# The lower part of streamed weights: a negative rounded copy by ScalarE and an adding transfer, in place of a subtraction by GpSimd

## The chip, the cores and the metric

The kernel runs on one core of one Trainium2 chip. The metric is the device time of one execution in microseconds (us). Three executions of the kernel before took 3351.83, 3354.24 and 3357.93 us; the median is 3354.24 us. Differences of about 0.2% (6.7 us) can be told apart.

## The reference

The kernel computes a small hybrid network for one sequence of 512 tokens of width 1024, in float32. It has two blocks of two layers each. Cut to what matters here:

```python
# block 1, two layers: two attentions side by side, then a gated feed forward with a convolution
h = rms_norm(x, attn_pre_gain);  u = h @ w_in                  # queries, keys, values, gates
o_a = swa_sink_attention(...)                                  # sliding window
o_b = nsa_attention(...)                                       # compressed, selected and window keys
mixed = sigmoid(g_a) * (o_a @ w_branch_a) + sigmoid(g_b) * (o_b @ w_branch_b)
x = x + rms_norm(mixed @ w_out, attn_post_gain)
h = rms_norm(x, ffn_pre_gain)
x = x + rms_norm(conv_ffn(h, w_up, conv_w, conv_b, w_down), ffn_post_gain)

def conv_ffn(h, w_up, conv_w, conv_b, w_down):                 # w_up: 1024 x 5632, w_down: 2816 x 1024
    u = h @ w_up
    c = conv_b + sum(conv_w[k] * shift(u, 2 - k) for k in range(3))
    a, val = split(c, 2);  return (gelu(a) * val) @ w_down

# block 2, two layers: a projection w_in_2, a convolution of width 7 over tokens and silu, a scan over the
# sequence in both directions in chunks of 128 tokens (ssd_chunked), a windowed attention, w_out_2, and the
# same kind of feed forward
```

Nearly all of the arithmetic is products of activations (512 tokens) with weight matrices. The weights are read once each.

## The kernel before

**Two parts of every number.** TensorE multiplies in a format that holds about half of a float32's significant bits (float32r in the program). So each weight is split into an upper part `wh`, the weight rounded to that format, and a lower part `wl = w - wh`; activations are split into `h` and `hl` (`ah` and `al` in the feed forward's second product) in the same way. A product of a 128x128 tile of weights with a 128x512 tile of activations is three matmuls into one PSUM bank, in `mm3`: L488 (`wh` by `h`), L489 (`wl` by `h`) and L490 (`wh` by `hl`).

**The stream of weights.** All weights lie in HBM in the order in which the kernel uses them (a table, PLAN), in 460 chunks of eight tiles: 128 partitions by 1024 float32, 512 KB. A class Stream takes them one after another. When the first tile of chunk c is asked for (`next`, L337), it first issues loads of raw chunks up to number c + 6 on SyncE's DMA queue (`load`, L301; four buffers `raw`), and then the conversions up to chunk c + 3 (`conv`; four buffers each of `wh` and `wl`). A conversion writes `wh` by a ScalarE copy that rounds (L314), or in the attention stages, 60 chunks of the 460, by a GpSimd cast (L312), since ScalarE is busy with exponentials there; then GpSimd subtracts: L315, `wl = raw - wh`. A chunk is 24 matmuls.

**The order.** Every engine works through its own list in the order in which the program's text issues the work, and waits where an operand isn't there. Other work is put between the matmuls by hand: `W.defer(n, f)` runs f after n more tiles of weights. So the place of the conversions in ScalarE's and GpSimd's lists is set by the calls of `next`.

**What the other engines do beside it.**
- Norms: ScalarE squares each of eight tiles (L416), VectorE adds them in turn (L421, the last one L424), TensorE sums over features with a column of ones (L433, `stat`). `dense_group` computes four output tiles of the next product meanwhile. L402 (ScalarE) and L403 (VectorE) make the two parts of the activations. After a post norm L1341 adds to x, on VectorE and GpSimd in turn.
- Feed forward: 22 pairs of output tiles of `w_up` in each of the four layers; 66 chunks of weights a layer, those of `w_down` among them. Each tile is evacuated by VectorE (L1224, `u`), convolved by ScalarE (L1228) and twice by VectorE (L1229, L1231); each pair then takes a gelu (L1250, ScalarE), a product (L1293, VectorE) and the split into `ah` (L1296, ScalarE) and `al` (L1298, VectorE). After thirteen pairs comes the first half of `w_down`.
- Block 2's convolution: GpSimd adds one tap (L1410), VectorE five (L1416), ScalarE applies silu (L1421), and TensorE transposes the result (L1520, `xtp`).
- The scan: GpSimd builds masked decays (L1628, `adm`) and weighted tiles (L1544, L1643, L1684), TensorE multiplies them (L1658, `gp`), VectorE forms the mixing tiles (L1662 to L1671), adds to the result (L1695, `xd`) and applies the gate z (L1704).
- Attention: scores on TensorE, exponentials on ScalarE (`p`, L1084 in block 1, L1938 in block 2), transposes of them on TensorE (L673, `pt`). In block 1 the gates of the branches are transposed once a layer (L1024, `gnt`, from `gn`, evacuated by VectorE at L811).

Of the kernel before, what the change touches and what calls it, by code (L numbers as in the profile page):

```python
# [23 lines left out]
NSLOT = 66              # working tiles of 128 x T  # L24
NB, NO = 2, 2           # output tiles taken together where the last factor comes late
XD = 30                 # tiles of weights before the first heads' queries are split
GA, GB, GC = 1, 4, 1    # tiles of weights before, between and within the gated products
NWU, NKW = 13, 6        # products that keep the clock up: at the start, at a norm
# [6 lines left out]
# ------------------------------------------------------------------ weight stream  # L35
# [8 lines left out]
def _plan():  # L44
    """128x128 weight tiles in the order in which the tensor engine takes them."""
# [103 lines left out]
# ------------------------------------------------------------------ constants of the shapes  # L149
# [37 lines left out]
def _onehot():  # L187
    """Bucket of each relative position -255..255 (t5, bidirectional); row 32 marks the outside."""
    oh = np.zeros((33, 512), np.float32)
    for i in range(512):  # L190
        rel = i - 255
        if i == 511 or abs(rel) > 128:
            oh[32, i] = 1
            continue
        n = abs(rel)
        b = n if n < 8 else 8 + sum(n * n >= 64 * 2 ** k for k in range(1, 8))
        oh[(16 if rel > 0 else 0) + min(b, 15), i] = 1
    return oh
# [48 lines left out]
def trunk_kernel(ctx: ExitStack, tc: tile.TileContext, xT, positions, wts, cst_d, oh_d, rb_d, cw1_d,  # L247
# [20 lines left out]
    # the eight banks of PSUM in turn; a bank that is held stays out until it is free again  # L268
# [16 lines left out]
    # ---------------------------------------------------------------- weights  # L285
    class Stream:
# [18 lines left out]
        def conv(self, upto):  # L305
            while self.conved < min(upto, NCHUNK):
# [3 lines left out]
                lo = wpool.tile([128, CH * 128], F32R, tag="wl", name="wl", bufs=4)  # L310
                if busy["act"]:
                    G.tensor_copy(h, r)  # L312
                else:
                    A.activation(h, r, AF.Copy)  # L314
                G.tensor_sub(lo, r, h.bitcast(F32))  # L315
# [3 lines left out]
        def defer(self, n, fn):  # L319
            """fn after n more tiles of weights."""  # L320
            self.later.append((self.t + n, fn))
# [26 lines left out]
        def drip(self, gen):  # L348
            """One step of gen for each tile of weights from now on."""
# [7 lines left out]
    # ---------------------------------------------------------------- constants  # L357
# [38 lines left out]
    def split(h, lo, src, eng_l=None, scale=None):  # L396
        """h + lo == src (times the column scale), each in 12 significant bits."""
# [7 lines left out]
    class Squares:  # L405
        """Squares summed over the feature tiles; the last tile stays one of its own where it comes late."""
# [19 lines left out]
        def sums(self, upto):  # L426
            """The sums over the features of a tile, [token of a block, block], for the tiles that are there."""
# [9 lines left out]
    def rstd_a(sq, n, act=False):  # L437
        """1/sqrt(mean + eps) of each token, [token of a block, block]."""
# [19 lines left out]
    def warm_sqrt():  # L458
        """Brings the table of the square root in ahead of its use."""
        A.activation(small(1, "warm"), epst, AF.Sqrt)  # L460

    def keep_warm(n):
        """Products that keep the tensor engine's clock up while it waits."""
# [4 lines left out]
    def spread(r4):  # L468
        """[token of a block, block] to [any partition, token], in PSUM."""
# [22 lines left out]
    def dense(keys, hs, evac):  # L492
        """One output tile; yields after each tile of the contraction."""
# [12 lines left out]
    def dense_parts(keys, hs, cut, evacs):  # L506
        """Some output tiles: the first part of the contraction for each of them, then the rest."""
# [11 lines left out]
    def dense_group(keys, hs, evacs, sq, store, x=None, after=None):  # L519
        """Four output tiles, the contraction outermost: it starts with the first tile of hs.  The factor of the  # L520
        norm (of the squares sq, of x where they are still to come) and what follows from it come a little into
        the next product."""
# [30 lines left out]
    def prep(x, gcol, late=False):  # L553
        """Gain and split of a tile, and its square for the norm; as a function of the tile's number."""
# [32 lines left out]
    def run_units(units, lags, fill, per, tail=0, prep=()):  # L587
        """Stage k of unit u comes at step u + lags[k]; the filler goes in between (per: steps per unit, tail:
        steps of the filler for each step after the last unit; prep: pieces of work, each with its first step)."""
# [25 lines left out]
    def pieces_of(gen, n):  # L615
        """A generator's n pieces as functions."""
        return [lambda: next(gen, None)] * n

    def stack_q(X, h, get):
        """One of a pair of heads as a tile of its two parts: products over all 128 rows; in two pieces."""  # L620
# [7 lines left out]
    def stack_k(K, g, get):  # L628
        """Keys of one of a pair of groups: their upper part and their lower part, each twice; in four pieces."""
# [19 lines left out]
    def head_units(h, score, ranges, order, vt, o, final):  # L649
        """The four units of a head: the scores of each block of queries; then for each block of keys (ranges: the  # L650
        queries that see it) the probabilities transposed, in two parts, and their product with the two parts of
        the values, side by side, over all those queries at once.  order: the keys, such that each of these
        products either adds to sums of all its queries or, the bank's marks cleared by the first one, starts them
        all.  o["t"][its half] becomes the
        product, [features, tokens]."""
# [57 lines left out]
    def widen(o, den):  # L713
        """A factor of each token, [token of a block, block and head], for each feature."""
# [3 lines left out]
    def spread_pair(o):  # L718
        """A pair of heads, [features, tokens], times their factors."""
# [11 lines left out]
    def value_parts(pt, s, name):  # L731
        """Values of one of a pair of groups, [tokens of a block, block, upper and lower part]."""
# [10 lines left out]
    # ================================================================ block 1  # L743
# [39 lines left out]
    def layer1(l, x, hs, sq, gnext, side):  # L783
# [48 lines left out]
        def tokens(src, name):  # L832
            """[features, tokens] to [tokens of a block, block, features]."""
# [5 lines left out]
        # ---- compressed keys and values  # L839
        cmp = {}  # L840

        def windows(src):
            """The tokens 16 n + 2 i + (0 or 1) of each group of heads, with the position added."""
# [70 lines left out]
        def cmp_scores(i):  # L914
            """Softmax over the compressed blocks, times the gate, transposed; all heads of a block."""
# [42 lines left out]
        def head(src, h):  # L958
            """The two pieces that make head h's tile; the source goes after the second head of the pair."""
# [7 lines left out]
        # ---- projections  # L967
# [63 lines left out]
        # ---- fillers  # L1031
# [20 lines left out]
        # ---- attention units  # L1052
# [10 lines left out]
        def halves(name):  # L1063
            """Half a tile; the other half goes to the next call."""
# [6 lines left out]
        def score_of(h, X, K, mask, k0, init, nm, den, last):  # L1071
            """Exponentials of the scores of a block of queries, not yet normed, and their first block of keys."""
# [16 lines left out]
        # sliding window with sinks  # L1089
# [42 lines left out]
        # selected blocks (all of them are selected) and window, both causal  # L1132
# [41 lines left out]
        # ---- branches, output, post norm  # L1174
# [40 lines left out]
        # ---- feed forward  # L1215
# [85 lines left out]
    def later(i, gated):  # L1301
        """The gated products of the pairs that are there, in steps a little into the products that follow."""
# [4 lines left out]
    class Acts:  # L1307
        """Eleven of the gated products, each taken when it is there."""
# [702 lines left out]
```

## Time and profile before

| | |
|---|---|
| median of three executions | 3354.24 us |
| span of the profiled execution | 3354.5 us |
| TensorE matmul (PE) busy | 3132.5 us, 93% |
| VectorE (DVE) busy | 2145.5 us, 64% |
| ScalarE (ACT) busy | 1465.3 us, 44% |
| GpSimd (POOL) busy | 1539.9 us, 46% |
| the 16 DMA engines, SyncE's queue | 303.50 MB, 28.7% of their time |
| read from HBM | 275.64 MB |

The span of the profiled execution is the time from its first to its last instruction and stands for the whole of it; it lies 0.3 us above the median. PE is TensorE's matmuls, PEld its loading of weights, SP is SyncE, which issues the loads of weights. Busy time is the time during which an engine executed something; time in which an instruction is held up after it has begun counts as busy. In rows "L315 POOL TENSOR_TENSOR wl<-wraw,wh" means: the instruction of line 315, on GpSimd, that writes `wl` from `wraw` and `wh`. A tile name of one letter, as `c`, `x` or `u`, is the working tile that the program calls so.

### The profile page before, as it was taken

The numbers are of one execution on the slowest core, as the hardware profiler recorded it, in microseconds if no ns is written. First come the engines' busy times: TensorE is split into PE (matmuls) and PEld (weight loads), VectorE is DVE, ScalarE is ACT, GpSimd is POOL, SyncE is SP. The second block draws the span as 40 slices with busy tenths as digits, with TensorE's granted clock in tenths as the row PEclk, the third lists the DMA queues.
The fourth block names the chain that finished last, engine by engine and source line by source line (L and its number), as shares of the span: only waits on it lengthen the run. The fifth ranks groups of instructions, "written<-read, shape, count | busy, mean of one in ns | idle before, by whom it ended". The sixth has DMA issues, their size and how long they took to land. (4 is left out here: it accounts for less than half of the span.)

```text
span 3354.5 us, 39917 instructions
## 1 busy us (share of the span) xinstructions
PE 3132.5 (93%) x14604; PEld 2567.9 (77%) x14604; DVE 2145.5 (64%) x3431; ACT 1465.3 (44%) x2828; POOL 1539.9 (46%) x770
## 2 busy tenths in 40 slices
PE   9989989999989999999888889999998888999998
PEld 7778778887778877888766667888887666788887
DVE  7787467263887747635578987462528898836253
ACT  3357344343246634433345466342333545734232
POOL 4533434554534334544447543354444664335443
PEclk8999999999999999999898899999999989999999
DMA  5311333333521133333321121333332102133332
GB/s 191 101 45 45 101 106 95 107 114 113 164 67 48 48 129 91 102 100 126 104 71 55 46 72 57 109 105 124 93 128 67 57 32 82 57 107 101 126 94 69
DMA packets 104031, 306.05 MB, mean 91 GB/s; under 512 B 12651, under 2 KB 21867, under 8 KB 103836
## 3 DMA queue, kind: packets, MB, share of 16 engines
q1 hardware_dynamic: 103836, 303.50, 28.7%
q8 instruction: 116, 1.90, 0.2%
q14 instruction: 79, 0.65, 0.1%
HBM read 275.64 MB, written 19.96 MB: 88 GB/s over the span
## 5 line engine op out<-in xcount | busy, mean ns | idle before, releaser
L315 POOL TENSOR_TENSOR wl<-wraw,wh 128x1024 fp32r<-128x1024 f32 x460 | 1165.2, 2538 | 1075.6 <-ACT wh L314 1006.4
L488 PE MATMUL acc<-h,wh 128*128 128x512 f32 x2464 | 1005.2, 408 | 0.7 <-ACT h L402 0.7
L489 PE MATMUL acc<-h,wl 128*128 128x512 f32 x2464 | 978.2, 397 | 2.5 <-POOL wl L315 2.5
L490 PE MATMUL acc<-hl,wh 128*128 128x512 f32 x2464 | 976.5, 396 | 0.2
L314 ACT ACTIVATE wh<-wraw 128x1024 fp32r<-128x1024 f32 x400 | 418.9, 1051 | 357.3 <-PE acc L490 257.9
L490 PEld LDWEIGHTS acc<-hl,wh 128*128 128x128 f32 x2464 | 473.1, 192 | 104.7 <-DVE hl L403 1.8
L489 PEld LDWEIGHTS acc<-h,wl 128*128 128x128 f32 x2464 | 474.6, 193 | 98.4 <-POOL wl L315 5.3
L488 PEld LDWEIGHTS acc<-h,wh 128*128 128x128 f32 x2464 | 475.0, 193 | 96.1 <-issue 5.0
L488 PE MATMUL acc<-ah,wh 128*128 128x512 f32 x704 | 274.4, 390 | 0.0
L490 PE MATMUL acc<-al,wh 128*128 128x512 f32 x704 | 274.1, 389 | 0.0
L489 PE MATMUL acc<-ah,wl 128*128 128x512 f32 x704 | 273.9, 389 | 0.0
L673 PE MATMUL pt<-cst,p 128*128 128x128 f32 x752 | 143.1, 279 | 34.1 <-DVE nm L1936 13.4
L1416 DVE SCALAR_TENSOR_TENSOR c<-u,prm,c 128x510 f32<-128x510 f32 (+2 forms) x120 | 147.9, 1233 | 40.8 <-POOL c L1410 37.4
L312 POOL CAST wh<-wraw 128x1024 fp32r<-128x1024 f32 x60 | 70.4, 1173 | 207.7 <-PE acc L490 207.5
L1298 DVE TENSOR_TENSOR al<-c,ah 128x512 fp32r<-128x512 f32 x88 | 118.0, 1341 | 70.8 <-ACT ah L1296 70.8
L490 PEld LDWEIGHTS acc<-al,wh 128*128 128x128 f32 x704 | 132.2, 188 | 28.5 <-DVE al L1298 0.9
L488 PEld LDWEIGHTS acc<-ah,wh 128*128 128x128 f32 x704 | 132.2, 188 | 27.8 <-ACT ah L1296 0.6
L489 PEld LDWEIGHTS acc<-ah,wl 128*128 128x128 f32 x704 | 132.2, 188 | 27.1
L421 DVE TENSOR_TENSOR sq<-sq 128x512 f32<-128x512 f32 x81 | 94.5, 1193 | 89.9 <-ACT sq L416 89.9
L1228 ACT ACTIVATE c<-u,prm 128x512 f32<-128x512 f32 x88 | 71.2, 815 | 163.8 <-DVE u L1224 163.8
L1084 ACT ACTIVATE p<-p,nm 128x128 f32<-128x128 f32 x192 | 102.5, 534 | 90.1 <-DVE nm L1082 88.2
L1296 ACT ACTIVATE ah<-c 128x512 fp32r<-128x512 f32 x88 | 55.5, 630 | 195.3 <-DVE c L1293 195.3
(333 smaller groups left out, 5313.7 us busy)
## 6 DMA issues: line engine op xcount, KB each, us to landing
wraw<-in_wts SPq DMA_DIRECT2D x460, 512.0 KB, 3.6
bias<-bias_d SPq DMA_DIRECT2D x32, 192.0 KB, 2.4
x<-in_xT SPq DMA_DIRECT2D x16, 256.0 KB, 6.1
cw<-in_cw SPq DMA_DIRECT2D x16, 256.0 KB, 4.4
xf<-x SPq DMA_DIRECT2D x16, 256.0 KB, 2.2
x<-xf SPq DMA_DIRECT2D x16, 256.0 KB, 5.6
xs<-x SPq DMA_DIRECT2D x16, 256.0 KB, 3.5
x<-xs SPq DMA_DIRECT2D x16, 256.0 KB, 6.0
```

Source lines behind the costliest of these rows:

```text
L312: G.tensor_copy(h, r)
L314: A.activation(h, r, AF.Copy)
L315: G.tensor_sub(lo, r, h.bitcast(F32))
L421: V.tensor_add(self.p[e], self.p[e], q)
L488: PE.matmul(acc, wh, xh, start=first, stop=False)
L489: PE.matmul(acc, wl, xh, start=False, stop=False)
L490: PE.matmul(acc, wh, xl, start=False, stop=last)
L673: PE.transpose(pt[:, 128 * n:128 * n + 128], t[:, 128 * (kb - b0):128 * (kb - b0) + 128], ident)
L1084: A.activation(p[:, 0:w], p[:, 0:w], AF.Exp, bias=nm[:, col:col + 1], scale=-1.0, accum_out=den[:, col:col + 1])
L1228: A.activation(c, u, AF.Identity, bias=cb[:, idx:idx + 1], scale=cw[:, 88 + idx:89 + idx])
L1298: V.tensor_sub(lo, a, h.bitcast(F32))
L1416: V.scalar_tensor_tensor(c[:, lo:hi], u[:, lo + d:hi + d], cw[:, 12 * k + idx:12 * k + idx + 1], c[:, lo:hi], op0=OP.mult, op1=OP.add)
```

## The change

`conv` makes the lower part in two other steps. ScalarE first writes `-w`, rounded, into `wl` (an activation with scale -1). Then GpSimd's DMA queue transfers the raw chunk from HBM again, straight onto `wl`, with an add at the destination: `wl = -round(w) + w`. The upper part is made behind that, as before. GpSimd's subtraction goes. The rest of the diff removes comments; from L316 of the changed kernel on, line numbers are one higher.

```diff
@@ class Stream, conv
                 h = wpool.tile([128, CH * 128], F32R, tag="wh", name="wh", bufs=4)
                 lo = wpool.tile([128, CH * 128], F32R, tag="wl", name="wl", bufs=4)
+                A.activation(lo, r, AF.Copy, scale=-1.0)
+                G.dma_start(out=lo, in_=wts[c], accum_op=OP.add)
                 if busy["act"]:
                     G.tensor_copy(h, r)
                 else:
                     A.activation(h, r, AF.Copy)
-                G.tensor_sub(lo, r, h.bitcast(F32))
                 self.hl[c] = (h, lo)
                 self.conved += 1
```

So there are 460 more activations on ScalarE, 460 DMAs issued by GpSimd, and 460 fewer subtractions on GpSimd. On TensorE, VectorE and SyncE the lists are the same.

ScalarE's list in the feed forward of the first layer (`c` the convolved tile, `ah` the upper part of the gated product), before:

```order
L1228 ACTIVATE c<-u,prm 128x512
L314 ACTIVATE wh<-wraw 128x1024
L1228 ACTIVATE c<-u,prm 128x512
L314 ACTIVATE wh<-wraw 128x1024
L1250 ACT_TABLE_LOAD
L1250 ACTIVATE c<-c 128x512
L1296 ACTIVATE ah<-c 128x512
```

and after the change:

```order
L1229 ACTIVATE c<-u,prm 128x512
L311 ACTIVATE wl<-wraw 128x1024
L316 ACTIVATE wh<-wraw 128x1024
L1229 ACTIVATE c<-u,prm 128x512
L311 ACTIVATE wl<-wraw 128x1024
L316 ACTIVATE wh<-wraw 128x1024
L1251 ACT_TABLE_LOAD
L1251 ACTIVATE c<-c 128x512
L1297 ACTIVATE ah<-c 128x512
```

Behind each convolution of a tile there now stand two conversions of a chunk, the lower part's first.

GpSimd's list in the scan of the third layer (`adm` masked decays, `xw` and `xd` weighted tiles), before:

```order
L315 TENSOR_TENSOR wl<-wraw,wh 128x1024 x2
L1628 TENSOR_TENSOR adm<-cst,adth 128x512
L1628 TENSOR_TENSOR adm<-cst,adtl 128x512
L1628 TENSOR_TENSOR adm<-cst,adth 128x512
L1628 TENSOR_TENSOR adm<-cst,adtl 128x512
L1544 TENSOR_TENSOR xw<-xtok,dtw 128x512 x2
L1643 TENSOR_TENSOR xd<-xtok,prm 128x512
L315 TENSOR_TENSOR wl<-wraw,wh 128x1024
L1684 TENSOR_TENSOR xd<-xd,yoff 128x512
```

and after the change:

```order
L312 DMA wl<-in_wts 128x1024 x2
L1629 TENSOR_TENSOR adm<-cst,adth 128x512
L1629 TENSOR_TENSOR adm<-cst,adtl 128x512
L1629 TENSOR_TENSOR adm<-cst,adth 128x512
L1629 TENSOR_TENSOR adm<-cst,adtl 128x512
L1545 TENSOR_TENSOR xw<-xtok,dtw 128x512 x2
L1644 TENSOR_TENSOR xd<-xtok,prm 128x512
L312 DMA wl<-in_wts 128x1024
L1685 TENSOR_TENSOR xd<-xd,yoff 128x512
```

The issue of a transfer stands where the subtraction stood; nothing else has moved. In the attention of block 1, where GpSimd makes the upper part too, its list before is:

```order
L315 TENSOR_TENSOR wl<-wraw,wh 128x1024
L312 CAST wh<-wraw 128x1024
L315 TENSOR_TENSOR wl<-wraw,wh 128x1024
L312 CAST wh<-wraw 128x1024
```

and after the change:

```order
L312 DMA wl<-in_wts 128x1024 x2
L314 CAST wh<-wraw 128x1024
L312 DMA wl<-in_wts 128x1024
L314 CAST wh<-wraw 128x1024
```

There the issue of the transfer now stands ahead of the cast of the same chunk, and waits for an activation on ScalarE that was not there before.

## Rows read from the trace of the kernel before

**Rows 1.** The page's first part: busy time, share and instructions of each engine.

```profile
span 3354.5 us, 39917 instructions
PE 3132.5 (93%) x14604; PEld 2567.9 (77%) x14604; DVE 2145.5 (64%) x3431; ACT 1465.3 (44%) x2828; POOL 1539.9 (46%) x770
```

**Rows 2.** Stretches of 84 us: feed forward of layer 1, convolution, scan.

```profile
core 0: us, PE busy (x) PEld busy (x) DVE busy (x) ACT busy (x) POOL busy (x), PEclk, DMA share, GB/s
588.00:672.00 84.00, 84.00 (x372) 69.60 (x371) 24.48 (x25) 29.72 (x37) 42.58 (x17) 1.00 0.34 106
1680.00:1764.00 84.00, 71.23 (x319) 57.92 (x318) 64.73 (x78) 35.47 (x64) 32.93 (x17) 0.94 0.23 73
1764.00:1848.00 84.00, 68.62 (x271) 50.30 (x270) 71.60 (x84) 47.01 (x121) 59.27 (x42) 0.90 0.16 51
```

**Rows 3.** Costly groups: count | busy us, mean ns | idle before, releaser.

```profile
L315 POOL TENSOR_TENSOR wl<-wraw,wh 128x1024 fp32r<-128x1024 f32 x460 | 1165.2, 2538 | 1075.6 <-ACT wh L314 1006.4
L489 PE MATMUL acc<-h,wl 128*128 128x512 f32 x2464 | 978.2, 397 | 2.5 <-POOL wl L315 2.5
L314 ACT ACTIVATE wh<-wraw 128x1024 fp32r<-128x1024 f32 x400 | 418.9, 1051 | 357.3 <-PE acc L490 257.9
L421 DVE TENSOR_TENSOR sq<-sq 128x512 f32<-128x512 f32 x81 | 94.5, 1193 | 89.9 <-ACT sq L416 89.9
L1231 DVE SCALAR_TENSOR_TENSOR c<-u,prm,c 128x510 f32<-128x510 f32 x88 | 106.4, 1209 | 3.1
L1293 DVE TENSOR_TENSOR c<-c 128x512 f32<-128x512 f32 x44 | 69.9, 1588 | 5.0 <-DVE c L1231 1.4
```

**Rows 4.** VectorE in order of time (start us, us, instruction), first feed forward.

```profile
547.26 0.75 DVE L1231 SCALAR_TENSOR_TENSOR c<-u,prm,c 128x510 f32<-128x510 f32 x1
...
550.87 2.76 DVE L1231 SCALAR_TENSOR_TENSOR c<-u,prm,c 128x510 f32<-128x510 f32 x1
```

**Rows 5.** GpSimd in the same stretch; in brackets idle before, and releaser.

```profile
547.47 2.81 POOL L315 TENSOR_TENSOR wl<-wraw,wh 128x1024 fp32r<-128x1024 f32 x1 [5.21 <-ACT wh L314]
550.49 2.59 POOL L315 TENSOR_TENSOR wl<-wraw,wh 128x1024 fp32r<-128x1024 f32 x1 [0.21 <-ACT wh L314]
```

**Rows 6.** TensorE in the same stretch: first use of the chunk's lower part.

```profile
550.66 0.39 PE L489 MATMUL acc<-h,wl 128*128 128x512 f32 x1
```

**Rows 7.** TensorE's waits, by releaser: us in total, times, longest.

```profile
PE xtp L1520 <- ACT c L1421: 28.0, 10, 7.8
PE stat L433 <- DVE sq L424: 26.7, 6, 7.5
PE gp L1658 <- DVE xd L1695: 21.2, 4, 8.2
PE gp L1658 <- DVE z L1704: 19.9, 6, 7.3
...
PE pt L673 <- ACT p L1938: 10.7, 14, 1.2
PE gnt L1024 <- DVE gn L811: 10.1, 2, 5.0
```

**Rows 8.** ScalarE at the norm ahead of the first feed forward.

```profile
451.94 1.04 ACT L314 ACTIVATE wh<-wraw 128x1024 fp32r<-128x1024 f32 x1
452.89 2.18 ACT L416 ACTIVATE sq<-x 128x512 f32<-128x512 f32 x4
```

**Rows 9.** GpSimd at the same norm.

```profile
453.11 2.40 POOL L315 TENSOR_TENSOR wl<-wraw,wh 128x1024 fp32r<-128x1024 f32 x1 [1.84 <-ACT wh L314]
```

**Rows 10.** VectorE at the same norm.

```profile
454.58 13.20 DVE L421 TENSOR_TENSOR sq<-sq 128x512 f32<-128x512 f32 x6 [1.76 <-ACT sq L416]
```

**Rows 11.** TensorE at the same norm.

```profile
468.56 1.87 PE L433 MATMUL stat<-ones,sq 128*128 128x1 f32 x8 [7.44 <-DVE sq L424]
```

**Rows 12.** The page's DMA issues: count, KB each, median us to landing.

```profile
wraw<-in_wts SPq DMA_DIRECT2D x460, 512.0 KB, 3.6
...
x<-in_xT SPq DMA_DIRECT2D x16, 256.0 KB, 6.1
```

**Rows 13.** VectorE in block 2's convolution, layer 3.

```profile
1713.25 6.02 DVE L1416 SCALAR_TENSOR_TENSOR c<-u,prm,c 128x510 f32<-128x510 f32 x5 [2.66 <-POOL c L1410]
```

**Rows 14.** TensorE at the start of the program.

```profile
8.13 0.50 PE L489 MATMUL acc<-h,wl 128*128 128x512 f32 x1 [0.78 <-POOL wl L315]
```

## The prediction

> **What bounds the kernel now.** I read four views. First the page's busy times: TensorE is busy 93% of the span of 3354.5 us, VectorE 64%, ScalarE 44%, GpSimd 46% [rows 1]. This is a TensorE kernel, and at most 3354.5 - 3132.5 = 222 us of idle TensorE can be won, besides clock. Second the same by stretches of 84 us [rows 2]: in the feed forward TensorE has 84.00 of 84 at granted clock 1.00, so nothing can be won there, only lost; in the stretches from 1680 to 1848 it has 71.23 and 68.62, at clock 0.94 and 0.90, while VectorE has 64.73 and 71.60. Third the costliest groups [rows 3]: the subtraction that goes, L315, is 460 instructions, 1165.2 us of GpSimd. Its price isn't its own time, since TensorE waits 2.5 us for it in all, ahead of L489. It is what VectorE does beside it. The same operation of VectorE (L1231) took 0.75 us at 547.26 and 2.76 us at 550.87 [rows 4]; the second began inside the subtraction that ran from 550.49 to 553.08 [rows 5] and ended only after it. The groups show it as means: L1293 1588 ns, L421 1193 ns, L1231 1209 ns. Against 0.75 us these three alone give 44 x 0.84 + 81 x 0.44 + 88 x 0.46 = 113 us of VectorE. Fourth, who ends TensorE's waits [rows 7]: the long ones end with VectorE, or with a ScalarE activation behind it (L1421).
>
> **The change part by part.**
>
> **1. The subtractions go; VectorE is no longer held up by them.** Each hold-up costs 2.76 - 0.75 = 2.0 us. I go through TensorE's waits in order of size.
> - Convolution, L1520 behind L1421: 28.0 us in 10 waits [rows 7]. In front of each stand five operations of L1416, 6.02 us at 1713.25 where 5 x 0.75 = 3.75 would do [rows 13]: 2.2 us to win per wait, 22 us if each wait is that long. Some are shorter; I take 18.
> - Norms, L433 behind L424: 26.7 us in 6 waits, the longest 7.5. At 468.56 the wait is 7.44 [rows 11], and in front of it six additions take 13.20 us [rows 10], where 6 x 0.75 = 4.5 would do. This place also pays for step 3, so its sum stands there.
> - Scan, L1658 behind L1695 and L1704: 21.2 + 19.9 = 41.1 us in 10 waits. One hold-up each would give 20 us. But GpSimd keeps its other work there, which starts earlier and meets VectorE again; I take 14, with 0 and 41 as ends.
> - L1024 behind L811: 10.1 us in 2 waits, one hold-up each: 4.
> - Clock: where TensorE pauses, the granted clock is 0.90 and 0.94, elsewhere 1.00 [rows 2]. If a third of the pauses goes in some eight such stretches, a third of 0.06 to 0.10 of 70 us comes back in each, 1.4 to 2.3 us, 11 to 18 us in all; part of it is spent waiting for VectorE. I take 8, with 0 and 25 as ends.
>
> What the issue of an accumulating transfer does to VectorE no row shows. Below it can do nothing, which is the sum above. Above, it could hold VectorE as long as the subtraction did, and the relief is 0. I take the first, since the hold-up in the rows comes with an operation that streams two tiles of 512 KB through GpSimd. The Trainium skill (SBUF — State Buffer, "Who interferes with whom") says that a VectorE instruction with two SBUF inputs contends with a GpSimd instruction that reads SBUF, not with one that only writes; the 2.76 us agree with the first half, no run shows the second yet. By that rule the relief is whole.
>
> **2. ScalarE gets 460 more activations** of the size of L314, 1.05 us each: 482 us, 44% to 58% of the span. In the feed forward that is 15.5 chunks (372 matmuls at 24) of 1.05 = 16 us beside 29.72 of 84 [rows 2]: there is room. In attention, where ScalarE so far left the weights to GpSimd, TensorE waits for its exponentials (L673 behind L1938, 10.7 us in 14 waits [rows 7]). If some 30 waits that end with ScalarE grow by a sixth of an activation, that is 5 us; ends 0 and 30 (all of them by a whole one).
>
> **3. The lower part comes by transfer and later.** So far it was ready 2.4 to 2.8 us after the upper part [rows 5, 9]. The raw chunk takes 3.6 us from issue to landing [rows 12]; the adding transfer brings the same 512 KB and must also read what it adds to. In the feed forward the engines' share is 0.34 at 106 GB/s [rows 2], of which a chunk per 84 / 15.5 = 5.42 us is 97 GB/s: 1.7 us of all 16 engines per chunk. I take 3.6 + 1.7 = 5.3 us after the negative part. Ends: 3.6 (adding is free) and 12.2 (twice an x tile's 6.1 for twice the bytes).
> - In the dense stretches conversion is called three chunks ahead, 3 x 5.42 = 16 us, and the transfer hides. But in the first feed forward it doesn't run that far ahead: the part that ended at 547.47 + 2.81 = 550.28 [rows 5] was used at 550.66 [rows 6]. With 5.3 us it would be 2.1 us late, were all else the same. What covers it: per pair of chunks VectorE's chain, for which ScalarE waits in order ahead of the conversions, gets shorter by at least the 2.0 us of step 1, while TensorE's 10.84 us per pair stay. The lead grows with each pair up to the three chunks that the buffers allow. I cost it at 0; without that cover it is 2.1 us per pair, see the rivals.
> - At the norms there is no lead. At 451.94 + 1.04 = 452.98 ScalarE has the first part [rows 8], the lower one was there at 455.51 [rows 9] and comes at 458.3, 2.8 us later. But TensorE waits 7.44 us further on, and that wait shrinks: the additions then follow the squares: behind 451.94 stand two pairs of activations (2 x 2.1) and eight squares (2.18 for four [rows 8]), 8.6 us, so 460.5, and with two last additions of 0.7 each 461.9. TensorE was there at 468.56 - 7.44 = 461.12; now it comes at 461.1 + 2.8 = 463.9 and goes on at once, 4.6 us ahead of 468.56. From 26.7 us I take three places like this one and a fourth with the 4.4 us that are left, where 1.6 come out: 3 x 4.6 + 1.6 = 15.
> - At the start TensorE waits until 8.13 [rows 14] for a part that a subtraction makes, of 2.4 us elsewhere [rows 9]. Among the loads of x an x tile takes 6.1 us [rows 12], half the bytes; 6.1 + 1.7 - 2.4 makes it 5 us later. Ends 1 and 10.
>
> **4. Order.** Beyond that no instruction changes places on TensorE or VectorE. On GpSimd the transfer stands where the subtraction stood; behind it wait the cast in attention and the products of the scan, as before. The queue of SP is the same.
>
> **Sum.** -18 (convolution) - 15 (norms, step 3 included) - 14 (scan) - 4 - 8 (clock) + 5 (ScalarE) + 5 (start) = -49 us. Against the profiled execution, 3354.5, that is 3305.5; the median of the runs is 3354.24, so I forecast 3305 us, 1.5% faster.
>
> **Rivals.**
> - **The adding transfer fills the DMA engines** (slower). A chunk now has 5.42 us, of which 0.34 is taken, so 3.6 us are left, 2.1 times the plain 1.7. If an adding row costs three times a plain one, a chunk needs 0.34 x 5.42 + 5.1 = 6.9 us instead of 5.42. Over the 264 feed-forward chunks (66 a layer) that is 1.5 x 264 = 390 us: 3700. It decides from 2.1 times on; at 2.3 times it is 0.3 x 264 = 80, so 3385. For it: three streams instead of two, in every stretch. Against: my estimate, counting streams, is 1.5 (three for two) to 2 plain transfers. The Trainium skill (Collectives: The Full Stack, "The bandwidth ceiling") gives a reduce with two source reads half the rate of a copy; by that, an estimate, a chunk takes 1.8 + 3.4 = 5.2 us, just inside.
> - **Lower parts late** (slower or as before): the lead doesn't grow, or the transfer takes nearer 12 us. At 2.1 us per pair, 11 pairs in each of the two first feed forwards, half as many in the others: 70 us, less the 49: 3375. For it: 0.38 us of slack at 550.66. Against: the relief sits in the very chain that makes the conversions late.
> - **No relief**: issuing transfers holds VectorE as the subtraction did, or takes GpSimd as long. Then only the 5 + 5 remain, and some of the waits: 3350 to 3365.
> - **More relief**: VectorE, with more than 113 us back, lets go of most waits in convolution, scan and norms: 28 + 41 + 27 + 10 and 20 of clock, less 10: 3240.
>
> **How the numbers follow.** Forecast 0.51 (own range 3275 to 3335); more relief 0.13; no relief 0.10; lower parts late 0.13; engines filled 0.13. A change of 0.2%, 6.7 us, is about what a measurement of this kernel can tell from none. Faster: 0.51 + 0.13 and 0.02 of no relief, 0.66; same: the rest of no relief, 0.08; slower: 0.26. The range from 3240 to 3410 leaves out most of the filled engines and a part below.
>
> **What would show it.** Right: L1293, L421 and L1231 fall to 0.7 to 0.8 us on average; VectorE's busy time falls by over 110 us, ScalarE's rises by 480; the waits at L433 shrink to under 3 us; the adding transfers land some 5 us after issue; DMA share about 0.8 in the feed forward with TensorE still at 84 of 84. Wrong: L489 waiting for transfers in the feed forward, with TensorE under 80 of 84, or VectorE's means unchanged.

## The result: 3261.66 us, 2.7% faster, and the profile after

The changed kernel takes 3261.66 us (median of four runs, 3260.16 to 3263.80), the kernel before 3354.31 us beside it: a ratio of 0.9726 with a 95% interval of 0.9712 to 0.9740, or 92.6 us less. The forecast was 3305 us, 49 us less, with a range of 3240 to 3410 us. The direction and the main mechanism were right, and the forecast size was a little over half of the measured one. The measured time lies below the forecast's own range (3275 to 3335 us, chance 0.51), between it and the rival "More relief" (3240 us, chance 0.13).

The page of the changed kernel, against [rows 1], [rows 3] and [rows 12]. From L317 on its line numbers are one higher than before; the two ways of making the upper part, L312 and L314 before, are L314 and L316 now. In the queue lines q0 is GpSimd's queue and q1 SyncE's (packets, MB, share of the 16 engines); the last two lines are DMA issues:

```profile
span 3261.3 us, 40685 instructions
...
PE 3097.5 (95%) x14604; PEld 2543.5 (78%) x14604; DVE 1752.6 (54%) x3431; ACT 1885.1 (58%) x3288; POOL 759.9 (23%) x770
...
q0 software_dynamic: 66240, 241.20, 43.5%
q1 hardware_dynamic: 103836, 303.50, 26.7%
...
L490 PE MATMUL acc<-h,wl 128*128 128x512 f32 x2464 | 971.7, 394 | 36.3 <-DMA wl<-in_wts 36.2
...
L312 POOL DMA_DIRECT2D wl<-in_wts x460 | 398.6, 866 | 2030.0 <-ACT wl L311 1837.0
L311 ACT ACTIVATE wl<-wraw 128x1024 fp32r<-128x1024 f32 x460 | 482.9, 1050 | 299.2 <-PE acc L490 271.9
...
wraw<-in_wts SPq DMA_DIRECT2D x460, 512.0 KB, 6.7
wl<-in_wts POOLq DMA_DIRECT2D x460, 512.0 KB, 7.1
```

VectorE does the same 3431 instructions in 393 us less. ScalarE works 420 us more: the new activations sum to 482.9 us, but the records of neighbours overlap by 0.1 us. GpSimd works 780 us less; of the 759.9 us that are left, 398.6 are the issues of the transfers (L312). The adding transfers take 43.5% of the DMA engines and land 7.1 us after issue; the plain loads beside them slow down from 3.6 to 6.7 us.

The groups of VectorE (count | busy us, mean ns | idle before, releaser) show where its 393 us went:

```profile
L1417 DVE SCALAR_TENSOR_TENSOR c<-u,prm,c 128x510 f32<-128x510 f32 (+2 forms) x120 | 98.5, 821 | 41.0 <-POOL c L1411 37.6
L1232 DVE SCALAR_TENSOR_TENSOR c<-u,prm,c 128x510 f32<-128x510 f32 x88 | 66.0, 750 | 3.1
...
L422 DVE TENSOR_TENSOR sq<-sq 128x512 f32<-128x512 f32 x81 | 53.8, 689 | 99.9 <-ACT sq L417 99.9
...
L1294 DVE TENSOR_TENSOR c<-c 128x512 f32<-128x512 f32 x44 | 30.5, 693 | 38.5 <-ACT c L1251 38.5
```

Against [rows 3] the means fall from 1209 to 750 ns, 1193 to 689 and 1588 to 693.

Stretches of 84 us (us; busy us and count of each engine; TensorE's clock, DMA share, GB/s): feed forward of layer 1, convolution, scan, against [rows 2]:

```profile
588.00:672.00 84.00, 84.00 (x373) 69.58 (x372) 17.74 (x25) 41.33 (x49) 12.95 (x15) 1.00 0.88 190
1660.00:1744.00 84.00, 84.00 (x386) 67.92 (x385) 58.16 (x87) 61.20 (x110) 30.43 (x32) 1.00 0.75 171
1740.00:1824.00 84.00, 61.64 (x256) 44.30 (x255) 79.22 (x117) 51.61 (x132) 45.85 (x44) 0.91 0.35 81
```

The feed forward is full at a DMA share of 0.88. The convolution, 71.23 of 84 before, is now full at full clock. The scan still has a quarter of its stretch open (61.64 of 84). The stretches after don't hold quite the same work as those before, since everything comes earlier; the stages below do.

TensorE's waits by releaser (us in total, times, longest), against [rows 7]:

```profile
PE acc L490 <- DMA wl<-in_wts: 36.2, 9, 6.6
PE gp L1659 <- DVE z L1705: 23.8, 6, 7.8
PE gp L1659 <- DVE xd L1696: 21.2, 4, 8.1
PE pt L674 <- ACT p L1939: 9.5, 18, 1.5
...
PE stat L434 <- DVE sq L425: 1.6, 4, 0.5
```

The convolution's 28.0 us are gone, and the norms' 26.7 us have become 1.6. New are 36.2 us for the adding transfer. The scan's 41.1 us became 45.0.

TensorE has the same 14604 matmuls in the same order in both traces, so each stage can be timed from the same matmul to the same matmul (us; idle is the sum of gaps on TensorE). The stages are cut by time in the trace before, so that a wait near a border can fall into the next row: the row of the feed forwards holds one wait behind a norm (4.9 us after the change, at 1618 us), and that of the scan the last two waits of layer 4's convolution (2.8 and 0.6 us before).

| stage | before | after | difference | idle, before to after |
|---|---|---|---|---|
| start, up to 50 us | 50.2 | 55.8 | +5.6 | 3.5 to 8.4 |
| attention, layers 1 and 2 | 748.5 | 711.9 | -36.6 | 47.1 to 21.2 |
| the norms ahead of and behind feed forwards | 193.5 | 184.5 | -9.0 | 33.7 to 22.6 |
| four feed forwards | 1428.3 | 1434.0 | +5.7 | 5.8 to 16.7 |
| convolution, both | 180.4 | 139.2 | -41.2 | 26.4 to 0.0 |
| scan, both | 309.7 | 299.5 | -10.2 | 58.3 to 57.4 |
| attention, layers 3 and 4 | 435.0 | 427.7 | -7.3 | 38.1 to 28.7 |

Idle TensorE fell from 213.0 to 155.0 us; another 35 us are matmuls that ran at a higher clock, since busy time fell from 3132.5 to 3097.5 us for the same matmuls.

### The profile page after: what moved, and what is told of

It reads as the page before. It is cut to its first block, busy times and chain, and to the rows that moved or that the text cites. A ratio compares the mean times of both kernels' runs of the same rounds, so it can differ in the third digit from the quotient of the medians.

```text
span 3261.3 us, 40685 instructions
## 1 busy us (share of the span) xinstructions
PE 3097.5 (95%) x14604; PEld 2543.5 (78%) x14604; DVE 1752.6 (54%) x3431; ACT 1885.1 (58%) x3288; POOL 759.9 (23%) x770
## 3 DMA queue, kind: packets, MB, share of 16 engines
q0 software_dynamic: 66240, 241.20, 43.5%
q1 hardware_dynamic: 103836, 303.50, 26.7%
## 5 line engine op out<-in xcount | busy, mean ns | idle before, releaser
L490 PE MATMUL acc<-h,wl 128*128 128x512 f32 x2464 | 971.7, 394 | 36.3 <-DMA wl<-in_wts 36.2
L489 PE MATMUL acc<-h,wh 128*128 128x512 f32 x2464 | 994.7, 404 | 0.8 <-ACT h L403 0.8
L312 POOL DMA_DIRECT2D wl<-in_wts x460 | 398.6, 866 | 2030.0 <-ACT wl L311 1837.0
L311 ACT ACTIVATE wl<-wraw 128x1024 fp32r<-128x1024 f32 x460 | 482.9, 1050 | 299.2 <-PE acc L490 271.9
L316 ACT ACTIVATE wh<-wraw 128x1024 fp32r<-128x1024 f32 x400 | 417.3, 1043 | 0.0
L674 PE MATMUL pt<-cst,p 128*128 128x128 f32 x752 | 144.0, 279 | 24.3 <-ACT p L1939 9.5
L1225 DVE TENSOR_TENSOR u<-acc,R 128x512 f32<-128x512 f32 x88 | 60.0, 687 | 173.3 <-PE acc L491 173.2
L680 ACT ACTIVATE pth<-pt 128x256 fp32r<-128x256 f32 (+2 forms) x320 | 130.7, 411 | 9.6 <-PE pt L674 7.1
L674 PEld LDWEIGHTS pt<-cst,p 128*128 128x128 f32 x752 | 93.3, 141 | 51.5 <-ACT p L1939 17.9
L1895 DVE TENSOR_TENSOR x<-x,acc 128x512 f32<-128x512 f32 x32 | 22.0, 688 | 185.3 <-PE acc L491 171.7
## 6 DMA issues: line engine op xcount, KB each, us to landing
x<-xf SPq DMA_DIRECT2D x16, 256.0 KB, 10.1
```

What stands on the lines that cost most here:

```text
L311: A.activation(lo, r, AF.Copy, scale=-1.0)
L312: G.dma_start(out=lo, in_=wts[c], accum_op=OP.add)
L489: PE.matmul(acc, wh, xh, start=first, stop=False)
L490: PE.matmul(acc, wl, xh, start=False, stop=False)
L674: PE.transpose(pt[:, 128 * n:128 * n + 128], t[:, 128 * (kb - b0):128 * (kb - b0) + 128], ident)
L680: A.activation(th[:, 0:w], pt[:, 0:w], AF.Copy)
```

## The experiments

The theories. A: VectorE is freed because GpSimd no longer reads two tiles beside it. B: what helps is that nothing in GpSimd's list or on TensorE waits for a subtraction any more. C: what counts is how busy GpSimd is. The experiments give each a number, and then price the transfer and the activations. Each kernel was timed beside the kernel before, whose medians were 3352.85 to 3355.64 us. Rows of experiments have line numbers shifted by the lines added.

**e3_pool_reads and e4_pool_writes: reading against being busy.** Both keep the change and give GpSimd work for which nothing waits:

```diff
 e3:
+                for k in (0, 512):
+                    G.tensor_sub(sp, r[:, k:k + 512], h[:, k:k + 512].bitcast(F32))
 e4:
+                for _ in range(5):
+                    G.memset(sp, 0.0)
```

> The changed kernel, and GpSimd again subtracts each chunk, in two halves into a tile that nobody reads, so nothing waits for the result. Theory A (VectorE is held up by GpSimd instructions that read): L1232, L422 and L1294 go back to 1.2 to 1.6 us and the time to 3330 to 3365 us. Theory B (the gain came from the lower part no longer being made by a subtraction that TensorE or GpSimd's list wait for): means stay at 0.7 to 0.8 us, 3261 to 3280 us.

> The changed kernel, and GpSimd fills a tile that nobody reads five times a chunk (memset of 128x512), so that it is busy but reads nothing. Theory A (reading is what holds VectorE up): VectorE's means stay at 0.69 to 0.80 us, time 3261 to 3285 us, more only through GpSimd's longer list. Theory C (any GpSimd work holds VectorE up, or GpSimd's list is what counts): means of 1 us and above and 3300 us or more.

Measured: 3396.36 us (ratio 1.0129, 1.0112 to 1.0146) for e3, 3252.53 us (0.9703, 0.9688 to 0.9718) for e4. Groups of e3, GpSimd's subtraction and three of VectorE's operations:

```profile
L319 POOL TENSOR_TENSOR sp<-wraw,wh 128x512 fp32r<-128x512 f32 x920 | 1338.0, 1454 | 41.8 <-issue 0.6
...
L1235 DVE SCALAR_TENSOR_TENSOR c<-u,prm,c 128x510 f32<-128x510 f32 x88 | 95.9, 1089 | 3.1
L425 DVE TENSOR_TENSOR sq<-sq 128x512 f32<-128x512 f32 x81 | 80.1, 1013 | 98.1 <-ACT sq L420 98.1
L1297 DVE TENSOR_TENSOR c<-c 128x512 f32<-128x512 f32 x44 | 80.1, 1820 | 10.6 <-ACT c L1254 6.4 <-DVE c L1235 0.9
```

TensorE's waits in e3 for the adding transfer and in the convolution:

```profile
PE acc L493 <- DMA wl<-in_wts: 38.6, 14, 7.4
PE xtp L1524 <- ACT c L1425: 30.3, 10, 7.5
```

The groups of e4:

```profile
L319 POOL MEMSET sp<- 128x512 f32 x2300 | 1366.1, 594 | 105.9
...
L1235 DVE SCALAR_TENSOR_TENSOR c<-u,prm,c 128x510 f32<-128x510 f32 x88 | 66.0, 750 | 3.1
L425 DVE TENSOR_TENSOR sq<-sq 128x512 f32<-128x512 f32 x81 | 53.8, 688 | 102.2 <-ACT sq L420 99.5 <-DMA wraw<-in_wts 2.7
L1297 DVE TENSOR_TENSOR c<-c 128x512 f32<-128x512 f32 x44 | 30.5, 692 | 38.6 <-ACT c L1254 38.6
```

GpSimd is as busy in the one (1338 us) as in the other (1366 us). Where it reads, VectorE's means go to 1.01 to 1.82 us and the time up by 135 us over the changed kernel; where it only writes, they stay at 0.69 to 0.75 us. In the two convolutions TensorE needs 139.2 us in the changed kernel, 182.3 in e3 and 141.5 in e4; the wait at L1520 of the kernel before (28.0 us) is back in e3 with 30.3. Later transfers aren't what makes e3 slow: TensorE waits 38.6 us for them, against 36.2 in the changed kernel. This settles it for A against B and C. The Trainium skill (SBUF — State Buffer, "Who interferes with whom") says just this: a VectorE instruction with two SBUF inputs contends with a GpSimd instruction that reads SBUF, not with one that only writes it. These runs agree with both halves. Both times missed their ranges: e3 came out above 3330 to 3365 us, probably because it pays for transfers and activations on top of the contention (no run separates these), and e4 came out 8 us below 3261 to 3285 us, with scans that are 20 us shorter, on which more under e6.

**e1_extra_act: the activations alone.** The kernel before, with `A.activation(lo, r, AF.Copy, scale=-1.0)` added ahead of each conversion.

> The kernel before, and ScalarE's negative activation added in front of each conversion (it writes wl, which the subtraction then overwrites); subtractions stay, no adding transfer. This prices the 460 activations alone. If the activations lie beside TensorE's work, as the prediction costed them (5 us, ends 0 and 30): 3354 to 3362 us, ScalarE's busy time up by about 480 us, the waits at L433 up by 1 to 2 us each. If ScalarE's longer list delays conversions and exponentials: 3370 to 3385 us, with more waiting at L673 and L489.

Measured: 3397.81 us (1.0137, 1.0122 to 1.0152), 45 us more and above either range. The waits of its TensorE that carry it:

```profile
PE acc L490 <- POOL wl L316: 21.1, 24, 2.0
...
PE acc L489 <- ACT ah L1297: 11.9, 2, 6.0
```

Two thirds of these 33 us lie in the first two feed forwards, which get 15 and 14 us longer. So without VectorE's relief the activations make lower parts and gated products late there. One caveat: of ScalarE's idle time ahead of the added activation 159.3 us end with GpSimd's subtraction, a wait that the changed kernel doesn't have, so 45 us may be too much for the activations alone.

**e2_no_add and e7_plain: the transfer.** e2 is the changed kernel without the transfer (the lower part stays -round(w)); e7 has the transfer without the add (it becomes a copy of w).

```diff
 e2:
-                G.dma_start(out=lo, in_=wts[c], accum_op=OP.add)
 e7:
-                G.dma_start(out=lo, in_=wts[c], accum_op=OP.add)
+                G.dma_start(out=lo, in_=wts[c])
```

> The changed kernel without the adding transfer (the lower part stays the negative rounded weight). This prices the transfer: its lateness and the traffic. If only the 36.2 us of waits at L490 for the transfer and about 10 us of slower other loads (cw, x) count: 3215 to 3230 us. If the waits only move to the next thing that is late (sums of squares, VectorE): 3240 to 3262 us. VectorE's means as in the changed kernel (0.69 to 0.75 us).

> The changed kernel with the same 460 transfers from GpSimd's queue but without the add (the lower part becomes a copy of the raw weights). It prices the add alone against the traffic. If the add is what lengthens them: packets of that queue take 22 to 27% of the engines' time for 241 MB in place of 43.5%, a transfer lands in 4 to 5 us in place of 7.1, raw chunks in 4 to 5 in place of 6.7, waits at L490 fall from 36 to 10 to 20 us, 3215 to 3240 us. If the second 512 KB of traffic and the queue are the cause: 6.5 to 7.5 us, 3250 to 3262 us.

Measured: 3177.81 us (0.9479, 0.9465 to 0.9493) for e2 and 3215.98 us (0.9582, 0.9569 to 0.9595) for e7. So the transfers with their issues cost the changed kernel 84 us, more than either range of e2 had: 38 for a second stream of plain transfers and 46 for the add. Queues, transfers and TensorE's wait in e7:

```profile
q1 hardware_dynamic: 103836, 303.50, 26.3%
q0 software_dynamic: 66240, 241.20, 25.7%
```

```profile
wraw<-in_wts SPq DMA_DIRECT2D x460, 512.0 KB, 4.5
wl<-in_wts POOLq DMA_DIRECT2D x460, 512.0 KB, 3.9
```

```profile
PE acc L490 <- DMA wl<-in_wts: 24.2, 5, 5.4
```

The same bytes take 25.7% of the engines without the add and 43.5% with it; by the spans that is 1.72 times as long, and a transfer lands in 3.9 us in place of 7.1. The Trainium skill (Collectives: The Full Stack, "The bandwidth ceiling") puts a reduce with two source reads at half the rate of a copy; measured here it is 0.58. Not all of this is traffic: the scans need 270.0 us in e2, 295.0 in e7 and 299.5 in the changed kernel, so 25 of the 38 us lie there. In e4, which has all the adding transfers, they need 279.4. What else the issues bring there comes under e6.

**e5_early: the norms.** In the changed kernel the chunk behind each norm is converted late. ScalarE at the norm ahead of the first feed forward (start us, us):

```profile
432.25 0.72 ACT L403 ACTIVATE h<-x,prm 128x512 fp32r<-128x512 f32 x1 [2.68 <-POOL x L1342]
432.88 1.04 ACT L311 ACTIVATE wl<-wraw 128x1024 fp32r<-128x1024 f32 x1
```

GpSimd's issue and TensorE's wait behind it:

```profile
434.22 0.88 POOL L312 DMA_DIRECT2D wl<-in_wts  x1 [2.01 <-ACT wl L311]
```

```profile
442.20 0.79 PE L490 MATMUL acc<-h,wl 128*128 128x512 f32 x1 [6.08 <-DMA wl<-in_wts]
```

The activation stands behind the last of the eight L403, and 7.9 us pass from issue to landing. The edit, in `post_norm`:

```diff
         r4 = rstd_a(sq, D, act=True)
+        W.conv(W.conved + 1)
```

> The changed kernel, but at each post norm one more chunk is converted ahead of the norm's own activations (W.conv(W.conved + 1) at its start, where the buffer of the chunk just finished is free). In the changed kernel's trace the four waits of 4.9 to 6.1 us at L490 behind the adding transfer (436, 816, 1230, 1613 us) follow an activation that stood behind the eight splits L403. If that place in ScalarE's list is the cause: those four waits fall from 22.4 us to under 6 and the time to 3238 to 3250 us. If the transfer's length is (7 to 8 us wherever it starts), or the sums of squares are then late: 3255 to 3262 us.

Measured: 3242.29 us (0.9666, 0.9653 to 0.9679), 19 us less. The waits at those four norms became 0.6, 2.5, 0.6 and 4.0 us, 7.7 together where under 6 was expected. A transfer still takes 7.0 us to land there (median). So the place in ScalarE's list was the cause, not the transfer's length alone.

**e6_memset and e6_scan: why the scan gained no idle time.** VectorE in the scan of the changed kernel:

```profile
1756.98 8.70 DVE L1669 TENSOR_SCALAR dm<-cbm,dt 128x128 f32<-128x128 f32 x1
1765.71 0.61 DVE L1670 SCALAR_TENSOR_TENSOR dm<-cbm,dt,dm 128x128 f32<-128x128 f32 x2
```

GpSimd beside it:

```profile
1757.07 1.57 POOL L1685 TENSOR_TENSOR xd<-xd,yoff 128x512 f32<-128x512 f32 x1
1758.30 1.33 POOL L1629 TENSOR_TENSOR adm<-cst,adth 128x512 fp32r<-128x512 f32 x1
1759.30 1.32 POOL L1629 TENSOR_TENSOR adm<-cst,adtl 128x512 fp32r<-128x512 f32 x1
...
1764.29 1.29 POOL L1644 TENSOR_TENSOR xd<-xtok,prm 128x512 f32<-128x512 f32 x1
```

An instruction that takes 0.28 us elsewhere took 8.70 us and ended 0.1 us after the last of a run of eight GpSimd products, which overlap by 0.3 us in the records. Ten instructions of L1669 are held 5.2 to 8.7 us in this way, and two of L1670, with two inputs, 6.9 us. Before, the same operation (L1668) was never over 2.33 us; VectorE got in while GpSimd's run went on:

```profile
1868.80 2.33 DVE L1668 TENSOR_SCALAR dm<-cbm,dt 128x128 f32<-128x128 f32 x1
```

```profile
1868.68 2.36 POOL L315 TENSOR_TENSOR wl<-wraw,wh 128x1024 fp32r<-128x1024 f32 x1
1871.01 1.03 POOL L1628 TENSOR_TENSOR adm<-cst,adth 128x512 fp32r<-128x512 f32 x1
1872.00 1.08 POOL L1628 TENSOR_TENSOR adm<-cst,adtl 128x512 fp32r<-128x512 f32 x1
```

e6_memset puts a one-column memset right behind each issue (`G.memset(tiny, 0.0)`), to see whether the issue ahead of the run is what matters. e6_scan lets ScalarE make the tiles of L1669:

```diff
-                        if hh % 2:
-                            A.activation(dm[:, sl], cbm[:, 128:256], AF.Copy, scale=d1)
-                        else:
-                            V.tensor_scalar(dm[:, sl], cbm[:, 128:256], d1, None, op0=OP.mult)
+                        A.activation(dm[:, sl], cbm[:, 128:256], AF.Copy, scale=d1)
```

> The changed kernel, and GpSimd writes one column (memset, 128x1) right behind each issue of an adding transfer. In the changed kernel's scan one single-input VectorE instruction (L1669) is held 5 to 9 us, for a whole run of GpSimd products that starts right behind an issue or behind each other; the kernel before never shows over 2.4 us. If the issue directly ahead is what lets the run keep VectorE out: L1669 no longer over 2.4 us, waits at gp 45 to about 30, 3245 to 3256 us. If the run itself does it: L1669 still 5 to 9 us, 3260 to 3270 us.

> The changed kernel, and in the scan ScalarE makes all of the tiles dm of which VectorE so far made every second one (L1669, the single-input instruction that is held up). If only the single-input instruction is kept out for a whole run of GpSimd's products: VectorE's next one, with two inputs, is held about 1 us at a time, the waits at gp fall from 45 to 20 to 25 us, 3238 to 3248 us. If any VectorE instruction is: L1670 and its like then show 5 to 9 us, waits at gp as before, 3258 to 3268 us.

Measured: 3259.25 us (0.9717, 0.9704 to 0.9731) for e6_memset, between its two ranges and no change that can be told apart, and 3240.59 us (0.9661, 0.9648 to 0.9674) for e6_scan, 21 us less. A row of VectorE in e6_memset:

```profile
1752.25 8.73 DVE L1671 TENSOR_SCALAR dm<-cbm,dt 128x128 f32<-128x128 f32 x1
```

and one in e6_scan:

```profile
1755.43 8.13 DVE L1667 SCALAR_TENSOR_TENSOR dm<-cbm,dt,dm 128x128 f32<-128x128 f32 x4 [1.47 <-ACT dm L1666]
```

So the issue directly ahead isn't it, and in e6_scan instructions with two inputs are held (up to 7.36 us for a single one): what stands first in VectorE's list when the run begins waits for its end. In e6_scan the waits at `gp` behind VectorE fall from 45.0 to 24.4 us; as the hold-ups are still there, this is put down to the work that ScalarE now does during them, which no run tests by itself. The time came as for the first theory, the mechanism as for the second. Why a run is let through whole here stays open. No VectorE instruction of that line is held over 1.3 us in e2, which issues no transfers, nor in e4, where five memsets follow each conversion, nor over 2.2 us in e3, where two subtractions do. e4's scans, without such hold-ups, are 20 us shorter than the changed kernel's. The add isn't needed for it, nor the overlap of the products: in e7, whose transfers don't add and whose products overlap by 0.04 us as before, VectorE shows

```profile
1722.66 8.47 DVE L1669 TENSOR_SCALAR dm<-cbm,dt 128x128 f32<-128x128 f32 x1
```

**e8_vector: VectorE subtracts.** The kernel before, with `V.tensor_sub` for `G.tensor_sub`.

> The kernel before, with the subtraction on VectorE in place of GpSimd (no adding transfer, no further activation). GpSimd no longer reads the weights, so by theory A VectorE's other instructions are freed as in the changed kernel, while its own list gets 460 subtractions of an estimated 1.4 us (twice the 0.69 us of L1294 for twice the columns), 640 us. If these lie beside TensorE's work except in convolution and scan (about 65 chunks, up to 90 us) and no transfer is late (84 us back): 3180 to 3260 us. If VectorE, waiting in order for ScalarE's upper part, becomes the bound of the feed forward: 3350 us and more.

Measured: 3301.04 us (0.9842, 0.9829 to 0.9855), between the two ranges. 460 subtractions of 1.25 us are 575 us of VectorE. Feed forwards and norms are as good as without transfers: the first feed forward needs 337.6 us, as in e2, and the norm ahead of it 32.9 (40.6 in the changed kernel). The convolutions need 183.0 us, 44 more than in the changed kernel, and the attention of layers 3 and 4 451.5 us, 24 more.

**e9_hybrid, e10_hybrid_scan and e11_best: each where it is best.** VectorE subtracts in the feed forwards and in the first twelve chunks of w_in (288 chunks), the adding transfer does the rest; e10 adds e6_scan's edit, e11 the first four chunks of w_in_2 in layer 3.

```diff
+                vec = DENSE[c]
+                if not vec:
+                    A.activation(lo, r, AF.Copy, scale=-1.0)
+                    G.dma_start(out=lo, in_=wts[c], accum_op=OP.add)
...
+                if vec:
+                    V.tensor_sub(lo, r, h.bitcast(F32))
```

> Stage by stage the better of two kernels: in the feed forwards and in the first twelve chunks of w_in of each layer of block 1 (288 chunks of 460) VectorE subtracts, elsewhere the adding transfer. From the stages of the changed kernel and of e8_vector: start 9 us, the four norms 8 + 3 + 8 + 9, layer 2's first projections 9, starts of the feed forwards 1.5 + 2.5 + 3 + 2, so 3261 - 55: 3200 to 3215 us if the stages add up; 3230 us and more if what a stage saves is waited for in the next.

> e9_hybrid, and the scan's tiles dm all by ScalarE as in e6_scan, where both scans took 9 us less each: 3182 to 3200 us if that adds to e9_hybrid; like e9_hybrid if not.

> e10_hybrid_scan, and the first four chunks of w_in_2 in layer 3 by VectorE too: its longest wait left for a transfer is 6.1 us at the norm ahead of them. If it goes as at the other norms: 3187 to 3195 us. If the sums of squares or VectorE are late there by then: 3194 to 3199 us.

Measured: 3213.22 us (0.9576, 0.9563 to 0.9589), 3197.07 us (0.9529, 0.9516 to 0.9542) and 3194.13 us (0.9517, 0.9504 to 0.9530). e9 and e10 lie in the first of their ranges: the stages add up. e11's 3 us over e10 are too few to be told from none. e11 is 2.1% below the changed kernel and 4.8% below the one before. Its longest waits are in the scan:

```profile
PE gp L1669 <- DVE z L1712: 13.8, 4, 5.3
PE gp L1669 <- DVE xd L1703: 10.5, 4, 4.0
PE pt L684 <- ACT p L1946: 9.8, 18, 1.5
```

## Why the prediction was right, and where it was short

- **VectorE's relief (step 1): right in kind.** The means that were to fall to 0.7 to 0.8 us fell to 0.69 to 0.75. e3 and e4 show the cause, reading and not being busy.
- **Convolution, -18: too small.** The stages gained 41.2 us. All 26.4 us of idle time went, where 18 was taken, and another 15 us came as clock; TensorE is at 1.00 there now, 0.94 before.
- **Clock, -8: too small.** Busy TensorE time fell by 35 us, above the 25 that the term had as its end; the 15 of the convolutions are among them. The term counted a third of the pauses in eight stretches; in the convolutions all pauses went.
- **Attention of layers 1 and 2: left out.** The sum had -4 (L1024, whose 10.1 us went whole) and +5 for ScalarE. The stages gained 36.6 us, 26 of them idle time. Its waits were below the size at which I stopped (2.3 to 3.4 us each, at 178, 223 and 382 us of the trace before and their like in layer 2), and the clock came on top. This and the convolution more than make up the 44 us that the forecast lacks.
- **Scan, -14: failed.** The step said that GpSimd's other work "meets VectorE again" and still took 14. The waits at `gp` rose from 41.1 to 45.0 us, since the hold-ups there come from GpSimd's own products, which now hold VectorE for a whole run (8.70 us). Step 1 had taken it that the issue of a transfer does nothing to VectorE; in the scan it does, since hold-ups of that length come only in kernels whose GpSimd issues transfers. The 10.2 us of the stages are nearly all clock; 3.4 us of idle time that went belong to the convolution's last transposes.
- **Norms, -15: came to -9.** The sums of squares are no longer late (26.7 to 1.6 us), but the transfer took 7.1 to 7.9 us where 5.3 was taken. That it has no lead there the step had said: its activation stands behind the splits of the norm, as L314 did. These four waits are 22.4 us where 4 x 2.8 was taken, and e5, which gives them a lead, took them away but for 7.7.
- **Start, +5: came to +5.6**, in one wait of 6.6 us.
- **ScalarE's activations, +5: not seen**, L674 waits 9.5 us where it waited 10.7. e1 suggests that this was owed to VectorE's relief, which the step didn't say: without it they cost up to 45 us. No run prices them in the changed kernel.
- **Lower parts late in the feed forwards, 0: +5.7.** The cover held in the main. VectorE's chain got shorter, as that step argued, and one chunk near the start of each feed forward was late, by 0.7 to 2.5 us, 7.2 in all.
- **The adding transfer:** an adding stream is 1.72 plain ones, inside the estimate of 1.5 to 2. It lands in 7.1 us where 5.3 was taken, beside raw loads that now take 6.7. The rival of full engines began to show, with a share of 0.88, but the feed forward stayed at 84.00 of 84. What that step lacked is the price elsewhere: e2 says 84 us in all for the transfers with their issues, most of it at the start, the norms, the scan (29.5 us, where the hold-ups are) and the first projections of layers 1 and 2.

So the forecast was short because the gains of VectorE's relief were summed from the longest waits alone, at partial credit, and by more than the costs were short. Of the costs the start and the feed forwards came near, and the transfer behind the norms was too cheap. Set against e2, both sides were far off: the kernel without transfers is 176 us faster than the one before, where the sum has 18 + 14 + 4 + 8 + 26.7 at the norms - 5 for ScalarE = 66, and the transfers take 84 us back, where it has 5 + 4 x 2.8 = 16. The two errors partly cancel; that the net of 49 came within a factor of two of 93 is in part luck.

## What to carry to other kernels

Where an engine slows down another, look for its price in the other's means: the same operation with and without the neighbour beside it gives the size, and the stages in which the slowed engine ends the waits give the gain, small waits and clock included. When work is moved off an engine, ask for each stage which engine has room: here the subtraction belongs to VectorE in the feed forward and to the DMA engines in the convolution, and the mix beat either by 2 to 3%. A transfer in place of an instruction needs its lead in the program's text, above all behind a norm, where the list that feeds it is blocked.

## What the runs showed of the hardware that was not expected

In the changed kernel a VectorE instruction was held for a whole run of GpSimd products (8.70 us against 0.28), where in the kernel before that operation was never held over 2.33 us. It comes with transfers issued by GpSimd, adding or plain (8.47 us in e7), and not where two subtractions or five memsets stand beside each issue (e3, e4); the cause is open. The Trainium skill (SBUF — State Buffer, "Who interferes with whom") speaks of a lock for one instruction; the trace shows a run of eight. An adding transfer of 512 KB costs 1.72 plain ones. And 2300 memsets on GpSimd, 1366 us of work, cost the kernel nothing on balance: e4 is 9 us faster than the changed kernel, with scans 20 us shorter.
